# A two-layer hybrid decoder step on one core: small parameters as one row, the constant table in two parts, and the first weights of layer 0 by halves of their rows

## The chip, the core and the metric

The kernel runs on one core of a Trainium2 chip. The core has TensorE (PE, with its weight loads PEld), VectorE (DVE), ScalarE (ACT), GpSimd (POOL) and SyncE (SP), and 16 DMA engines that move data between device memory and the on-chip memories. SP and POOL also issue transfers: each has a queue of its own, and transfers of one queue are issued in the order of the program. The metric is the time of one execution on the device, in microseconds (us).

## The reference

Two decoder layers run over 256 prompt tokens and 8 sample tokens, model width 1024, all in float32. In each layer one wide projection `u = x @ w_in` feeds three token mixers (retention, state-space, sliding-window attention). Gates from the same `u` mix their results, an output projection, a layer norm and a gated feed-forward block follow. What the change touches is the start of the first layer: which columns of `w_in` are used there, and the small vectors of one number per head.

```python
(q_r, k_r, v_r, g_r, z, xbc, dt_raw, q_c, k_c, v_c, gates) = split(x @ w_in)
dt = softplus(dt_raw + dt_bias);  a = -exp(a_log)          # 16 heads
y  = ssd(...) + d_skip[:, None] * xs                       # 16 heads
# sliding-window attention: 8 query heads, 2 key heads of 64, window 128
bias   = rel_bias[t5_bucket(max(dist, 0))]                 # 32 buckets x 8 heads
logits = where(mask, q_c . k_c / 8 + bias, -1e30)
p = softmax(concat([logits, sinks], -1))[..., :-1];  o_c = p @ v_c
```

## The kernel before

The 264 token columns lie along the free dimension: `x` is kept transposed as eight blocks of 128 rows by 264 columns. Since products in full float32 are wanted, each float32 operand is split into a rounded part and a rest (`xh`, `xl` for the data, `wh`, `wl` for the weights), and each block product is three matmuls (`mm3`): wh by xh, wh by xl, wl by xh, each 128x128 weights by 264 columns. One output block of 128 columns of `w_in` (a unit, PSUM tile `ps_u`) is 8 blocks, so 24 matmuls.

Weights come in strips of 1 MB (256 columns of `w_in`, two units) on SP's queue (`strip`), into a pool of four buffers. For each unit `wsplit` makes `wh` on ACT (line 139, a rounded copy) and `wl` on DVE (line 144, a subtraction). Small loads go on POOL's queue (`ld`, line 167).

Layer 0 starts like this. `load_x` loads the first 128 columns of the constant table `cst` (an identity matrix) and x; PE transposes x by blocks (`ps_x`, line 127), ACT and DVE split each block (`xsplit`). Then come the units in this order: `w_kv` (2 units: keys and values of the attention), `w_qc` (4 units: its queries), `w_v` (4 units), `w_qk` (8 units). The strips of `w_qc` are gathered by two head groups each, so each strip is two transfers of 0.5 MB with runs of 128 numbers (512 bytes). The rest of `cst`, 1.1 MB, is loaded on SP's queue behind `w_qc` and ahead of `w_v` (`load_const`). `params` loads the vectors of a layer: 100 rows of 128 numbers (`par_rows`), which PE transposes at once (`ps_par`), and the vectors of one number per head (`dt_bias`, `a_log`, `d_skip`, `sinks`) by broadcasting loads into 128 partitions (`head`). `params` of layer 1 runs early in layer 0's mixers.

The attention needs a bias table. `bias_table` builds 8 rows of 383 numbers in `brow`, from the 32x8 bucket table (matmul `ps_rb`), writes them to device memory (`bias_row`), copies them there into 128 shifted places per head (`bias`, two copies of 766 KB), and loads the shifted table back as `bias_t` (two loads of 512 KB). The score tiles `ps_sc` on PE are read by DVE (`lg<-ps_sc,bias_t`, line 156), which adds the bias; the score tiles come from a pool of four PSUM buffers (`psm`), so later score matmuls wait until DVE has read earlier ones.

The order on each engine is fixed when the program is built: a list scheduler sorts the instructions by the program's order, by priorities (`high_priority`) and by explicit "not before" links (`issue_after`). Some generators (bias table, attention, layer 1's parameters) are put on a list and advanced in pieces by `pump` between units.

Of the kernel before, what the change touches and what calls it, by code (L numbers as in the profile page):

```python
# [10 lines left out]
F32 = mybir.dt.float32  # L11
# [8 lines left out]
DEPTH = 2  # L20
# [10 lines left out]
NEG = -1e30  # L31
RSCALE = 128**-0.5
CONV = 1536

# [70 lines left out]
class Kern:  # L105
# [87 lines left out]

    def wsplit(self, raw, shape):

        n = int(np.prod(shape))
        pool = self.hps[self.nsplit % len(self.hps)]
        self.nsplit += 1
        h, l = (pool.tile([128, 1024], F32R, tag=t, bufs=3 if pool is self.hp else 1, name=t) for t in ("wh", "wl"))
# [11 lines left out]
        return hv, lv  # L211

    def mm3(self, ps, wh, wl, xh, xl, first, last):
# [14 lines left out]

    def gemm_kouter(self, ws, x, pss):
        n = len(x)  # L230
        for k in range(n):
            for (wh, wl), ps in zip(ws, pss):
                self.mm3(ps, wh[:, k], wl[:, k], x[k][0], x[k][1], k == 0, k == n - 1)


    def load_x(self):
        nc, a, cp = self.nc, self.a, self.cp
        keep = _OFF["onehot"][0]
        self.cst = cp.tile([128, keep], F32, name="cst")
        nc.sync.dma_start(self.cst[:, 0:128], a["cst"][:, 0:128])  # L240

# [6 lines left out]
        nc.sync.dma_start(xt[1], a["x_prompt"][0, 128:256])  # L248
        nc.sync.dma_start(xs, a["x_sample"][:, 0])
        bias = self.bias_table()  # L250
# [11 lines left out]
        self.neg = cp.tile([128, 128], F32R, name="neg")  # L262
# [4 lines left out]
        nc.vector.memset(self.neg.bitcast(F32), -1.0 / 128)  # L267
        nc.vector.memset(self.eps[:, 0:1], EPS)
        nc.vector.memset(self.eps[:, 1:2], 4.0 * EPS)

    def load_const(self):
        nc, a = self.nc, self.a
        keep = _OFF["onehot"][0]
        nc.sync.dma_start(self.cst[:, 128:], a["cst"][:, 128:keep])
        self.par = [None] * DEPTH

    def params(self, l):

        nc, a, cp = self.nc, self.a, self.cp
        rows = self.T2("par_rows")[:100, :128]  # L280
        q = self.ld
# [12 lines left out]
        q(hd[:, 16:32], a["a_log"][l].partition_broadcast(128))  # L294
        for s in range(2):
            q(
                hd[s * 64 : s * 64 + 64, 32:40],
                a["d_skip"][l].rearrange("(h s) -> s h", s=2)[s].partition_broadcast(64),
            )
        q(hd[:, 40:48], a["sinks"][l].partition_broadcast(128))  # L300
        self.act(hd[:, 16:32], hd[:, 16:32], AF.Exp)
        self.par[l] = (t, hd)
# [242 lines left out]
    def mixers(self, l):  # L545
# [9 lines left out]

        def units(c0, n, name, done, kouter=False, unnormed=False):
            for i in range(0, n, 2):
                raw = self.strip([(0, 128, self.win(l, c0 + i * 128, 256))], (8, 256), name)
                if unnormed:
                    for u in range(2):  # L560
                        done(i + u, self.unnormed(self.wsplit(ucol(raw, u), (8, 128)), u > 0))
                    continue
                if kouter and i == 0:
                    ws = [self.wsplit(ucol(raw, u), (8, 128)) for u in range(2)]
                    pss = [self.pg("ps_u") for _ in range(2)]
                    self.gemm_kouter(ws, self.x, [p[:, :T] for p in pss])
                    for u in range(2):
                        done(u, pss[u])
                    continue
# [9 lines left out]

        kv = self.kv = self.E2("kv")  # L580
        units(KC, 2, "w_kv", lambda u, ps: self.act(kv[:, u * T : (u + 1) * T], ps[:, :T]), l == 0, l > 0)
        qc = self.qc = self.E4("qc")
        wq = a["w_in"][l][:, QC : QC + 512].rearrange("(k p) (g c) -> p k g c", p=128, g=2)
        for i in range(2):
# [5 lines left out]
            if l == 0 and i == 1:  # L590
                self.load_const()
                self.params(0)
            for u in range(2):
                t = 2 * i + u
                w = self.wsplit(raw[:, :, :, u * 64 : (u + 1) * 64], (8, 2, 64))
                if l > 0:
                    ps = self.unnormed(w)
                else:
                    ps = self.pg("ps_u")
                    self.gemm(w, self.x, ps[:, :T])  # L600
                self.act(qc[:, t * T : (t + 1) * T], ps[:, :T])
                self.pump(1)
# [3 lines left out]
        self.ld(rd, self.win(l, DT, 16))  # L606
        self.conv_prep(l)
        self.rate = 1.5
        vr = self.vr = self.E4("vr")
        put = lambda u, ps: self.act(vr[:, u * T : (u + 1) * T], ps[:, :T])  # L610
        units(VR, 2, "w_v", put, False, l > 0)
        if l > 0:
# [463 lines left out]
    def swa(self, l):  # L1076
# [97 lines left out]
        KT3 = KT[:, :1024].rearrange("p (b n) -> p b n", b=8)  # L1174
        self.ld(kc3, a["cache_swa_k"][l].rearrange("b w g d -> w b (g d)"))
        self.ld(vc3, a["cache_swa_v"][l].rearrange("b w g d -> w b (g d)"))
# [74 lines left out]
    def ret(self, l):  # L1251
# [37 lines left out]
        def load_state(h):  # L1289
            s0 = self.SI("rs0")[:, :1024]  # L1290
            self.ld(s0.rearrange("p (b v) -> p b v", b=8), a["state_ret"][l][:, h].rearrange("b k v -> k b v"))
            loaded.append(s0)
# [352 lines left out]
```

## Time and profile before

| | us |
|---|---|
| three timed runs | 1118.53, 1124.67, 1124.10 |
| their median | 1124.1 |
| the profiled execution | 1120.48 |
| its span, from the first to the last instruction | 1118.7 |
| around the span (1120.48 less 1118.7) | 1.8 |
| PE busy | 1085.1 (97%) |
| DVE, ACT, POOL busy | 838.8, 660.8, 165.6 |

The profile is of one execution. Busy times of the engines overlap. The granted clock of TensorE in the profiled execution is 0.988 of full speed as a mean. The chain of work that ended last is followed back from the last instruction; 89% of it are PE's instructions.

### The profile page before, as it was taken

The numbers are of one execution on the slowest core, as the hardware profiler recorded it, in microseconds if no ns is written. First come the engines' busy times: TensorE is split into PE (matmuls) and PEld (weight loads), VectorE is DVE, ScalarE is ACT, GpSimd is POOL, SyncE is SP. The second block draws the span as 40 slices with busy tenths as digits, with TensorE's granted clock in tenths as the row PEclk, the third lists the DMA queues.
The fourth block names the chain that finished last, engine by engine and source line by source line (L and its number), as shares of the span: only waits on it lengthen the run. The fifth ranks groups of instructions, "written<-read, shape, count | busy, mean of one in ns | idle before, by whom it ended". The sixth has DMA issues, their size and how long they took to land.

```text
span 1118.7 us, 22107 instructions
## 1 busy us (share of the span) xinstructions
PE 1085.1 (97%) x8583; PEld 1032.6 (92%) x8583; DVE 838.8 (75%) x1898; ACT 660.8 (59%) x1318; POOL 165.6 (15%) x250
## 2 busy tenths in 40 slices
PE   6799999999999999999999999999999999999998
PEld 5788899998899999999998899989899999999996
DVE  3178685688968998777699769668886799777654
ACT  3147553767664686664457855456666558766452
POOL 5010001242000101222011000133100000122300
PEclk9889999999999999999999999999999999999999
DMA  9874445588455668899775445659766536889941
GB/s 212 217 259 151 130 138 167 187 218 260 144 188 156 193 219 287 288 299 336 223 229 173 152 138 153 173 145 273 213 189 203 171 122 223 286 290 306 323 177 40
DMA packets 179977, 230.78 MB, mean 206 GB/s; under 512 B 8056, under 2 KB 156160, under 8 KB 179696
## 3 DMA queue, kind: packets, MB, share of 16 engines
q1 hardware_dynamic: 159472, 166.95, 47.2%
q0 software_dynamic: 20336, 62.39, 19.7%
q8 instruction: 67, 1.10, 0.4%
q14 instruction: 38, 0.31, 0.1%
q10 hardware_dynamic: 64, 0.03, 0.0%
HBM read 213.57 MB, written 19.61 MB: 208 GB/s over the span
## 4 chain that ended last, share of the span: by engine, by line
PE 89%; DVE 4%; DMA 4%; ACT 2%; issue 1%; SPq 0%; ACTq 0%
PE ps_u L123 18%; PE ps_gate L123 13%; PE ps_fd L123 11%; PE ps_fg L123 9%; PE ps_fu L123 9%; PE ps_br L123 8%; PE ps_z L123 5%; PE ps_o L123 4%; DMA w_v<-in_w_in_dram 3%; PE ps_y L123 2%; DVE wl L144 1%; PE ps_po L123 1%; ACT wh L139 1%; PE ps_var L123 1%; DVE xl L156 1%
## 5 line engine op out<-in xcount | busy, mean ns | idle before, releaser
L123 PE MATMUL ps_u<-xh,wh 128*128 128x264 f32 x608 | 179.0, 296 | 9.9 <-ACT wh L139 9.9
L123 PE MATMUL ps_u<-xl,wh 128*128 128x264 f32 x608 | 177.4, 292 | 0.0
L123 PE MATMUL ps_u<-xh,wl 128*128 128x264 f32 x608 | 176.6, 293 | 0.5 <-DVE wl L144 0.5
L123 PEld LDWEIGHTS ps_u<-xh,wh 128*128 128x128 f32 x608 | 117.6, 194 | 15.1 <-ACT wh L139 11.3
L123 PEld LDWEIGHTS ps_u<-xh,wl 128*128 128x128 f32 x608 | 117.7, 194 | 3.7 <-issue 1.8
L123 PEld LDWEIGHTS ps_u<-xl,wh 128*128 128x128 f32 x608 | 117.9, 194 | 2.6 <-issue 2.1
L123 PE MATMUL ps_gate<-xh,wh 128*128 128x264 f32 x384 | 111.2, 293 | 4.5 <-ACT th L139 3.2
L123 PE MATMUL ps_gate<-xh,wl 128*128 128x264 f32 x384 | 110.6, 291 | 0.0
L123 PE MATMUL ps_gate<-xl,wh 128*128 128x264 f32 x384 | 110.1, 290 | 0.0
L123 PE MATMUL ps_fd<-fh,wl 128*128 128x264 f32 x352 | 100.4, 285 | 0.0
L123 PE MATMUL ps_fd<-fh,wh 128*128 128x264 f32 x352 | 100.3, 285 | 0.0
L123 PE MATMUL ps_fd<-fl,wh 128*128 128x264 f32 x352 | 100.1, 284 | 0.0
L144 DVE TENSOR_TENSOR wl<-w_fd,wh 128x1024 fp32r<-128x1024 f32 (+1 forms) x48 | 54.2, 1135 | 38.6 <-ACT wh L139 38.3
L123 PE MATMUL ps_fg<-xh,wh 128*128 128x264 f32 x288 | 82.1, 285 | 0.6 <-DVE v L156 0.6
L123 PE MATMUL ps_fg<-xl,wh 128*128 128x264 f32 x288 | 82.5, 286 | 0.0
L123 PE MATMUL ps_fu<-xh,wh 128*128 128x264 f32 x288 | 82.5, 286 | 0.0
L167 POOL DMA_DIRECT2D s<-in_state_ssm_dram x32 | 28.7, 898 | 361.0 <-ACT sn L139 223.7
L123 PE MATMUL ps_fu<-xl,wh 128*128 128x264 f32 x288 | 82.1, 285 | 0.0
L123 PE MATMUL ps_fg<-xh,wl 128*128 128x264 f32 x288 | 81.8, 284 | 0.0
L123 PE MATMUL ps_fu<-xh,wl 128*128 128x264 f32 x288 | 81.8, 284 | 0.0
L139 ACT ACTIVATE wh<-w_gate 128x1024 fp32r<-128x1024 f32 x48 | 50.7, 1059 | 48.4 <-PE ps_br L123 17.8
L139 ACT ACTIVATE wh<-w_fd 128x1024 fp32r<-128x1024 f32 (+1 forms) x48 | 47.2, 986 | 53.7 <-PE ps_fd L123 44.6
(454 smaller groups left out, 3431.9 us busy)
## 6 DMA issues: line engine op xcount, KB each, us to landing
w_gate<-in_w_in_dram SPq DMA_DIRECT2D x24, 1024.0 KB, 5.5
w_fg<-in_w_ffn_gate_dram SPq DMA_DIRECT2D x22, 1024.0 KB, 5.3
w_fu<-in_w_ffn_up_dram SPq DMA_DIRECT2D x22, 1024.0 KB, 5.6
s<-in_state_ssm_dram POOLq DMA_DIRECT2D x32, 512.0 KB, 7.0
w_fd<-in_w_ffn_down_dram SPq DMA_DIRECT2D x16, 1024.0 KB, 9.4
out_dram<-sn POOLq DMA_DIRECT2D x24, 512.0 KB, 7.7
w_qk<-in_w_in_dram SPq DMA_DIRECT2D x8, 1024.0 KB, 5.2
w_xs<-in_w_in_dram SPq DMA_DIRECT2D x8, 1024.0 KB, 5.3
```

The costliest lines, as they stand in the source:

```text
L123: return self.nc.tensor.matmul(out, lhsT, rhs, start=start, stop=stop).ins
L139: i = self.nc.scalar.activation(out=out, in_=in_, func=func, scale=scale, **kw)
L144: return self.nc.vector.tensor_tensor(out=out, in0=a, in1=b, op=op).ins
L156: return self.nc.vector.scalar_tensor_tensor(out=out, in0=a, scalar=s, in1=b, op0=op0, op1=op1).ins
L167: return self.nc.gpsimd.dma_start(out, in_).ins
```

## The change

- **Vectors per head.** `params` no longer loads `dt_bias`, `a_log`, `d_skip` and `sinks` by broadcast. Four loads of 16, 16, 16 and 8 numbers put them into one row beside `par_rows`; one matmul of a row of ones with that row (`ps_head`) spreads them over 128 partitions, and ACT copies them out into `head`. Layer 1's `params` now runs near the end of layer 0.
- **Constant table.** The first load takes 256 columns (identity and ones) instead of 128; the rest is loaded later in the program's text, in SP's queue still behind `w_qc` and ahead of `w_v`.
- **First weights by halves of rows.** In layer 0, `w_kv` and `w_qc` are loaded as two strips each that hold rows 0 to 511 and 512 to 1023: two of 0.5 MB with 1 KB runs, two of 1 MB with 2 KB runs. `wsplits` splits 512 numbers a row at a time into halves of a `wh`/`wl` pair. All units of a strip's first half run before its second half.
- **Warm-up.** 32 matmuls of 128x128 on a constant tile (`neg`) are put on PE ahead of the transposes.
- **Splits of x.** They get a priority of 400. The bias row is pumped after all eight blocks of x, with `issue_after` links that put the loads of the retention state (`rs`) behind the load of the key cache.

```diff
+WARM = 32
@@ load_x
-        nc.sync.dma_start(self.cst[:, 0:128], a["cst"][:, 0:128])
+        nc.sync.dma_start(self.cst[:, 0:256], a["cst"][:, 0:256])
...
+        ps = self.pg("ps_warm")
+        for _ in range(WARM):
+            self.mm(ps[:, :128], self.neg, self.neg)
...
         for k in range(KB):
-            if k == KB - 1:
-                self.pump(1)
...
-            self.xsplit(*self.x[k], ps[:, :T])
+            with self.tc.high_priority(400):
+                self.xsplit(*self.x[k], ps[:, :T])
+        self.pump(1)
@@ params
-        q(hd[:, 0:16], a["dt_bias"][l].partition_broadcast(128))
...
+        row = slot[:1, 128:184]
+        for nm, o, n in (("dt_bias", 0, 16), ("a_log", 16, 16), ("d_skip", 32, 16), ("sinks", 48, 8)):
+            q(row[:, o : o + n], a[nm][l : l + 1])
+        ph = self.pm("ps_head")
+        self.mm(ph[:, 0:56], self.c("ones")[0:1], row)
@@ wsplits, new
+        t = [self.hp.tile([128, 1024], F32R, tag=t, bufs=3, name=t) for t in ("wh", "wl")]
+        return [self.wsplit(r, shape, tuple(x[:, i * n : (i + 1) * n] for x in t)) for i, r in enumerate(raws)]
@@ halves, new
+            pss = [self.pg("ps_u") for _ in range(n)]
+            for i in range(2):
+                raw = self.strip([(0, 128, self.win(l, c0, n * 128)[:, 4 * i : 4 * i + 4])], (4, n * 128), name)
+                for u in range(0, n, 2):
+                    ws = self.wsplits([pieces(raw, u + v) for v in range(2)], shape)
+                    if n == 2:
...
+                                self.mm3(pss[v][:, :T], *(w[:, k] for w in ws[v]), *x, i + k == 0, i == 1 and k == 3)
...
+                        self.gemm(ws[v], self.x[4 * i : 4 * i + 4], pss[u + v][:, :T], i == 0, i == 1)
@@ mixers, layer 0
+            for u, ps in enumerate(halves(KC, 2, "w_kv", ucol, (4, 128))):
+                put_kv(u, ps)
...
+            pss = halves(QC, 4, "w_qc", head, (4, 2, 64))
+            self.params(0)
@@ load_state
+            with self.tc.issue_after(self.kv_ld):
+                self.ld(s0.rearrange("p (b v) -> p b v", b=8), a["state_ret"][l][:, h].rearrange("b k v -> k b v"))
```

On ACT, at the very start of the program, before:

```order
L139 ACTIVATE xh<-ps_x 128x264 x5
L139 ACTIVATE wh<-w_kv 128x1024 x2
L139 ACTIVATE xh<-ps_x 128x264 x2
L139 ACTIVATE wh<-w_qc 128x1024
L139 ACTIVATE xh<-ps_x 128x264
```

and in the same place now:

```order
L141 ACTIVATE wh<-w_kv 128x512 x4
L141 ACTIVATE xh<-ps_x 128x264 x4
L141 ACTIVATE wh<-w_qc 128x512 x2
L141 ACTIVATE xh<-ps_x 128x264 x4
L141 ACTIVATE wh<-w_qc 128x512 x2
```

All four copies of `w_kv` stand ahead of the first `xh`, and two copies of `w_qc` ahead of the other four; before, five of the eight `xh` stood ahead of any weights. DVE has its subtractions in the same order.

On POOL's queue, behind the last row of `par_rows`, before (`head_313` is layer 0's, `head_4391` layer 1's):

```order
L167 DMA head_313<-in_d_skip_dram 64x8x1 x2
L167 DMA head_313<-in_sinks_dram 128x8
L167 DMA w_dt<-in_w_in_dram 128x8x16
L167 DMA cst_rows<-in_state_conv_dram 24x1536
...
L167 DMA rs_1629<-in_state_ret_dram 128x8x128
L167 DMA rs_1840<-in_state_ret_dram 128x8x128
L167 DMA head_4391<-in_dt_bias_dram 128x16
L167 DMA bias_row<-brow 8x383
L167 DMA head_4391<-in_a_log_dram 128x16
L167 DMA head_4391<-in_d_skip_dram 64x8x1 x2
L167 DMA head_4391<-in_sinks_dram 128x8
L167 DMA bias<-bias_row 512x1x383 x2
```

and in the same place now, up to the load of the key cache and the states:

```order
L169 DMA par_rows<-in_d_skip_dram 1x16x1
L169 DMA par_rows<-in_sinks_dram 1x8x1
L169 DMA w_dt<-in_w_in_dram 128x8x16
L169 DMA cst_rows<-in_state_conv_dram 24x1536
...
L169 DMA bias_row<-brow 8x383
L169 DMA bias<-bias_row 512x1x383 x2
L169 DMA bias_t<-bias 128x4x256 x2
L169 DMA kcache<-in_cache_swa_k_dram 128x8x128
L169 DMA rs_1679<-in_state_ret_dram 128x8x128
L169 DMA rs_1890<-in_state_ret_dram 128x8x128
```

Layer 1's broadcast loads and the loads of the states no longer stand ahead of the bias row and the bias copies.

On PE, around the score tiles of the third and fourth head, before (`ps_u_663` is the second unit of `w_qk`):

```order
L123 MATMUL ps_u_663<-xh_84,wl_660 128x264
L123 MATMUL ps_sc_547<-kv_169,qc_232 128x128
L123 MATMUL ps_sc_547<-kv_169,qc_232 128x256
L123 MATMUL ps_u_663<-xh_84,wh_659 128x264
L123 MATMUL ps_sc_548<-kv_169,qc_232 128x128
```

and now (`ps_u_571` and `ps_u_611` are the third and the fourth unit of `w_v`):

```order
L125 MATMUL ps_u_571<-xh_84,wl_568 128x264
L125 MATMUL ps_sc_597<-kv_202,qc_203 128x128
L125 MATMUL ps_sc_597<-kv_202,qc_203 128x256
L125 MATMUL ps_sc_598<-kv_202,qc_203 128x128
L125 MATMUL ps_sc_598<-kv_202,qc_203 128x256
L125 MATMUL ps_u_611<-xh_84,wh_607 128x264
```

The fifth and sixth score tile, which take buffers that DVE must first have read with the bias table, moved from 93 matmuls of `ps_u` behind the first eight score matmuls to 24 behind them.

## Rows read from the trace of the kernel before

**Rows 1.** The page, busy time, share of the span and instructions of each engine.

```profile
PE 1085.1 (97%) x8583; PEld 1032.6 (92%) x8583; DVE 838.8 (75%) x1898; ACT 660.8 (59%) x1318; POOL 165.6 (15%) x250
```

**Rows 2.** The chain that ended last, in order of time: start us, us, what.

```profile
20.50 34.49 DMA w_v<-in_w_in_dram
...
60.26 13.19 PE ps_u L123 x93
...
417.09 2.95 PE ps_fu L123 x24
```

**Rows 3.** PE's timeline: start us, us, instruction [idle before <-releaser].

```profile
12.03 0.59 PE L123 MATMUL ps_u<-xh,wh 128*128 128x264 f32 x1
...
28.37 0.39 PE L123 MATMUL ps_u<-xh,wh 128*128 128x264 f32 x1 [3.63 <-ACT wh L139]
...
45.35 0.59 PE L123 MATMUL ps_u<-xh,wh 128*128 128x264 f32 x1 [5.54 <-ACT wh L139]
...
56.78 1.43 PE L123 MATMUL ps_sc<-kv,qc 64*128 64x128 f32 x6 [1.70 <-ACT convbuf L139]
```

**Rows 4.** Stretches: PE, PEld, DVE, ACT, POOL busy (instructions), PEclk, DMA share, GB/s.

```profile
30.00:35.00 5.00, 5.00 (x31) 5.00 (x30) 1.06 (x3) 0.13 (x2) 1.05 (x1) 0.68 1.11 176
45.00:50.00 5.00, 4.20 (x17) 3.89 (x18) 2.45 (x2) 1.80 (x4) 0.00 (x0) 0.50 0.59 214
55.00:60.00 5.00, 3.12 (x15) 1.86 (x14) 3.66 (x13) 4.81 (x10) 1.38 (x3) 0.71 1.06 345
60.00:70.00 10.00, 10.00 (x68) 9.81 (x67) 4.06 (x4) 2.77 (x5) 3.25 (x5) 0.81 0.94 324
8.00:10.00 2.00, 1.37 (x8) 0.93 (x8) 1.45 (x4) 1.27 (x5) 1.16 (x3) 1.00 1.13 347
14.00:16.00 2.00, 2.00 (x11) 2.00 (x10) 1.50 (x4) 1.06 (x1) 2.00 (x3) 1.00 1.39 92
18.00:20.00 2.00, 2.00 (x18) 2.00 (x17) 0.31 (x1) 0.01 (x1) 0.54 (x1) 1.00 0.80 0
50.00:52.00 2.00, 2.00 (x18) 1.96 (x17) 0.00 (x0) 0.00 (x0) 0.00 (x0) 0.94 0.53 190
```

**Rows 5.** ACT's timeline, columns as in rows 3: splits of the weights.

```profile
10.74 2.00 ACT L139 ACTIVATE wh<-w_kv 128x1024 fp32r<-128x1024 f32 x2 [0.39 <-DMA w_kv<-in_w_in_dram]
...
27.26 1.06 ACT L139 ACTIVATE wh<-w_qc 128x1024 fp32r<-128x1024 f32 x1 [4.73 <-DMA w_qc<-in_w_in_dram]
...
44.24 1.06 ACT L139 ACTIVATE wh<-w_v 128x1024 fp32r<-128x1024 f32 x1 [14.12 <-DMA w_v<-in_w_in_dram]
...
55.09 1.06 ACT L139 ACTIVATE wh<-w_v 128x1024 fp32r<-128x1024 f32 x1 [8.29 <-DMA w_v<-in_w_in_dram]
```

**Rows 6.** SP's timeline, the time its queue took to issue (SPq).

```profile
2.98 9.15 SPq L191 DMA_DIRECT2D w_qc<-in_w_in_dram  x4
12.17 5.32 SPq L274 DMA_DIRECT2D cst<-in_cst_dram  x1
17.53 9.83 SPq L188 DMA_DIRECT2D w_v<-in_w_in_dram  x2
```

**Rows 7.** Transfers issued by POOL: count, KB each, median us from issue to landing.

```profile
head<-in_d_skip_dram POOLq DMA_DIRECT2D x1, 2.0 KB, 15.8
...
bias_row<-brow POOLq DMA_DIRECT2D x1, 12.0 KB, 14.5
...
bias<-bias_row POOLq DMA_DIRECT2D x1, 766.0 KB, 20.9
...
bias_t<-bias POOLq DMA_DIRECT2D x2, 512.0 KB, 6.8
```

**Rows 8.** POOL's timeline, columns as in rows 3: the steps of the bias table.

```profile
18.80 0.54 POOL L167 DMA_DIRECT2D bias_row<-brow  x1 [2.65 <-DVE xl L144]
...
33.95 2.26 POOL L167 DMA_DIRECT2D bias<-bias_row  x2 [5.54 <-DMA bias_row<-brow]
...
60.81 1.56 POOL L167 DMA_DIRECT2D bias_t<-bias  x2
```

More of the change, by code (lines that the diff above doesn't have):

```diff
@@ L192, in strip, with wsplit @@
         return v
-    def wsplit(self, raw, shape):
+    def wsplit(self, raw, shape, into=None):
         n = int(np.prod(shape))
-        pool = self.hps[self.nsplit % len(self.hps)]
-        self.nsplit += 1
-        h, l = (pool.tile([128, 1024], F32R, tag=t, bufs=3 if pool is self.hp else 1, name=t) for t in ("wh", "wl"))
+        if into is None:
+            pool = self.hps[self.nsplit % len(self.hps)]
+            self.nsplit += 1
+            into = tuple(pool.tile([128, 1024], F32R, tag=t, bufs=3 if pool is self.hp else 1, name=t) for t in ("wh", "wl"))
+        h, l = into
         spec = {2: "p (a b) -> p a b", 3: "p (a b c) -> p a b c"}[len(shape)]
@@ L249, in load_x @@
         nc.sync.dma_start(xs, a["x_sample"][:, 0])
+        self.neg = cp.tile([128, 128], F32R, name="neg")
+        nc.vector.memset(self.neg.bitcast(F32), -1.0 / 128)
+        self.par = [None] * DEPTH
+        ps = self.pg("ps_warm")
+        for _ in range(WARM):
+            self.mm(ps[:, :128], self.neg, self.neg)
         bias = self.bias_table()
@@ L554, in unit, with halves, units @@
             return ps
-        def units(c0, n, name, done, kouter=False, unnormed=False):
+        def halves(c0, n, name, pieces, shape):
+            pss = [self.pg("ps_u") for _ in range(n)]
[4 more added lines that the diff above has]
+                    if n == 2:
+                        for k in range(4):
+                            for v in range(2):
+                                x = self.x[4 * i + k]
+                                self.mm3(pss[v][:, :T], *(w[:, k] for w in ws[v]), *x, i + k == 0, i == 1 and k == 3)
+                        continue
+                    for v in range(2):
+                        self.gemm(ws[v], self.x[4 * i : 4 * i + 4], pss[u + v][:, :T], i == 0, i == 1)
+            return pss
+        def units(c0, n, name, done, unnormed=False):
             for i in range(0, n, 2):
@@ L561, in units @@
                         done(i + u, self.unnormed(self.wsplit(ucol(raw, u), (8, 128)), u > 0))
[L562 to L568, printed above, removed]
                     continue
@@ L580, in mixers @@
         kv = self.kv = self.E2("kv")
-        units(KC, 2, "w_kv", lambda u, ps: self.act(kv[:, u * T : (u + 1) * T], ps[:, :T]), l == 0, l > 0)
+        put_kv = lambda u, ps: self.act(kv[:, u * T : (u + 1) * T], ps[:, :T])
         qc = self.qc = self.E4("qc")
+        put_qc = lambda t, ps: self.act(qc[:, t * T : (t + 1) * T], ps[:, :T])
         wq = a["w_in"][l][:, QC : QC + 512].rearrange("(k p) (g c) -> p k g c", p=128, g=2)
-        for i in range(2):
+        if l == 0:
+            for u, ps in enumerate(halves(KC, 2, "w_kv", ucol, (4, 128))):
+                put_kv(u, ps)
+            head = lambda raw, t: raw.rearrange("p k (g t d) -> p k g t d", g=2, t=4)[:, :, :, t]
+            pss = halves(QC, 4, "w_qc", head, (4, 2, 64))
+            self.params(0)
+            for t, ps in enumerate(pss):
+                put_qc(t, ps)
+                self.pump(1)
+        else:
+            units(KC, 2, "w_kv", put_kv, True)
+        for i in range(2 if l else 0):
             raw = self.strip(
@@ L589, in mixers @@
             )
-            if l == 0 and i == 1:
-                self.load_const()
-                self.params(0)
             for u in range(2):
[L594 to L601, printed above, removed]
+                put_qc(2 * i + u, self.unnormed(self.wsplit(raw[:, :, :, u * 64 : (u + 1) * 64], (8, 2, 64))))
                 self.pump(1)
@@ L607, in mixers @@
         self.conv_prep(l)
+        if l == 0:
+            self.load_const()
         self.rate = 1.5
@@ L610, in mixers @@
         put = lambda u, ps: self.act(vr[:, u * T : (u + 1) * T], ps[:, :T])
-        units(VR, 2, "w_v", put, False, l > 0)
+        units(VR, 2, "w_v", put, l > 0)
         if l > 0:
```

30 lines of the change are left out of this document (11 added, 19 removed).

## The prediction

> **What bounds the kernel now.** I read the page first: PE is busy 97% of the span [rows 1], so only PE's gaps and its slow stretches are to be had. The chain in order of time says where they lie [rows 2]: one wait for `w_v` fills it from 20.50 to 54.99, and from about 60 us on PE runs almost without a break. So the change, which rewrites the first 60 us and a few instructions of layer 1, is worth what PE loses before that.
>
> PE's timeline gives the idle part [rows 3]: 3.63 us before 28.37 (second strip of `w_qc`, whose split starts at 27.26), 5.54 before 45.35 (first strip of `w_v`, split from 44.24 [rows 5]) and 1.70 before 56.78, where the score matmul waits for a buffer that ACT empties late, behind a split that waits for the second `w_v` strip (55.09 [rows 5]). Together 10.9 us.
>
> The clock gives the other part. At the full level 24 matmuls of a unit take 2.95 us [rows 2], 0.123 each. After each of the gaps the granted clock fell, to 0.50 of 2.4 GHz, that is 1.2 GHz, in parts of the stretches shown [rows 4]: 31 matmuls in 30 to 35 where 41 would fit (1.2 us lost); 17 in 4.20 busy us in 45 to 50 (2.1 lost); 3.12 busy us at a mean of 0.71 in 55 to 60 (0.9); 68 in 60 to 70 where 81 would fit (1.7). Sum 5.9 us. What is recoverable behind the start is thus 10.9 + 5.9 = **16.8 us**.
>
> Why do the strips come late? Not by their size. The transfers run at 347 GB/s in 8 to 10, then at 92 in 14 to 16 and at 0 in 18 to 20 with the engines still 80% busy [rows 4]. In that time the broadcast loads were in flight: 2 KB of `d_skip`, 512 elements of 4 bytes each with a stride of two, take up to 15.8 us to land [rows 7]. SP itself needed 9.15 us to issue the four transfers of `w_qc`, 5.32 for the table, 9.83 for two `w_v` strips [rows 6]. So I take the small-element loads to be what held the strips; the trace doesn't separate them from the 512-byte runs of `w_qc`, and the change removes both.
>
> **The change part by part.**
>
> *Vectors as a row, and `w_qc` by halves.* Four broadcast loads go, and the four of layer 1 leave this stretch. Bytes ahead of and with the first `w_v` strip on SP's queue: x 1.1 MB, table 0.13 and 1.1, `w_kv` 1.05, `w_qc` 2.1, strip 1.05: 6.5 MB. At 324 GB/s (60 to 70 [rows 4]) that is 20 us, at 285 it would be 23, and 2 us pass before the first transfers: with both: the first `w_v` strip is there at 22 to 25 instead of 44.24. The second half of `w_qc` comes at about 18. PE reaches `w_v` at about 35 (below), so 10 us of cover stand over the first wait: 3.63 and 5.54 go in full. If the flow stayed as bad as 92 GB/s for another 6 us, the cover would still hold. New on PE: one `ps_head` matmul, on ACT four more evacuations of 8 to 16 columns; ACT is idle 14.12 us before 44.24 [rows 5], so nothing for these.
>
> *`w_kv` by halves, splits behind weights.* The code puts the splits of x first by priority, but the order now has ACT do all four `w_kv` copies first, and they need the second half of `w_kv`. A copy of a whole unit takes about 1.0 us (2.00 for two [rows 5]), half a unit about 0.5. The same 1 MB lands as before, about 10.7 [rows 5]; two half copies more, one `xh`: first `ps_u` at about 12.3 against 12.03 [rows 3]. Bounds: 11.5, if the halves land earlier, to 14; I take **0.3 us lost**. Four blocks of x stay behind the first `w_qc` half (about 14.6, copies until 15.7): PE has 24 matmuls at the slow spacing to run by then (5 us, until 17.5), so no wait.
>
> *Warm-up.* 32 matmuls of 128 columns at no more than 0.22 us each (the spacing of a 264-column matmul there) are 7.2 us from about 1, done by 8.2; the transposes begin then, but ACT takes the first `xh` now only at about 12, and the last transpose needed for it is done by 11.5. Cost 0 for that, up to 0.5 if the memset is late. Gain: in 14 to 16 PE did 11 matmuls in 2 us and in 18 to 20 it did 18 [rows 4], so the start runs at the lower level, 18 matmuls from 12.03, 1.8 us lost. After the gap of 3.63 us the clock fell again [rows 3, 4]; between the end of the warm-up and 12.3 PE has only transposes with gaps. By the row nothing is left of the warmth: I take 0, range 0 to 1.8. The Trainium skill ("TensorE: Matmul & The Clock Gate", "What's actually happening") says that the slow state is the default and that activity lifts it, by which the warm-up would be worth the 1.8 us; no run here shows that yet.
>
> *Second `w_v` strip and the emptying of buffers.* In the new order PE's transposes of k and v for the sample rows (`ps_cts`), between the first and second unit of `w_v`, wait for a buffer that ACT empties behind its third `w_v` copy, so behind the second `w_v` strip. That strip landed 10.85 us after the first (55.09 less 44.24 [rows 5]), while the bias copies ran; by the same distance it is there at 33 to 36, at a stretch with worse flow (190 GB/s at a share of 0.53 in 50 to 52 [rows 4]) at 38. PE is through the first unit at 38.2. A copy of 1.06 and one small evacuation follow: **1.0 us lost**, bounds 0 and 4. The wait of 1.70 before 56.78 goes in exchange.
>
> *Bias row early, states late.* This edit pays nothing by itself and creates a new wait. The row is written at about 18.8 as before [rows 8], behind all splits of x; it took 14.5 us to land [rows 7] with the broadcast and state loads ahead, now perhaps 5.5: about 24.4. The copies then took 20.9 [rows 7]. They move 3.1 MB both ways, 14.5 us at the 214 GB/s of 45 to 50 [rows 4]. So `bias` lands at 39 to 45 and `bias_t` 6.8 us later [rows 7] plus issue, at 46.5 to 54. But the third and fourth heads' score tiles now stand on PE between the third and the fourth unit of `w_v` and need buffers that DVE frees with `bias_t`. PE gets there at about 46. Queued behind that wait on PE: the fourth `w_v` unit and all of `w_qk`; on DVE, behind the same bias table, the second `w_qk` subtraction. I take `bias_t` at 47.5: **1.5 us lost**, bounds 0 and 8, with the clock's fall afterwards 0 to 2.
>
> *Rest.* Layer 1's parameters at the end of layer 0, and states after the key cache: small orders in stretches where PE runs on other work; 0, bounds -0.5 and +2.
>
> **The sum.** PE: first unit 12.3, `w_kv` done 21.8 (with the four transposes and the bias-row matmuls inside), `w_qc` 96 x 0.123 later, 34, transposes 35.3, first `w_v` unit 38.2, wait 1.0, second 42, eight score matmuls, third 46, wait 1.5, fourth, scores, first `w_qk` unit about 55; 21 matmuls of the next, 57.8. Before, that point was 73.45 (60.26 + 13.19, 93 matmuls after the scores [rows 2]), with 0.9 us of score matmuls not yet done: this way 16 us. By losses: 16.8 removed, less 0.3, 1.0 and 1.5: 14.0. I go by the second, which is the surer, with half a microsecond of the first: 14.5. The profiled execution of 1120.48 less 14.5 is **1106**. Against the median of the runs, 1124.1, which lies 3.6 above it, the same gain would give 1109.6; the profile's own execution is between the three, so I stay with 1106 and let the range hold the other.
>
> **The rivals.**
>
> 1. *The bias table is late.* The copies take 20.9 us again or more, since the weight strips now flow beside them: `bias_t` at 53 to 55, PE waits 7 to 9 us at the fifth score tile and runs slowly for some us after it. Gain 14.5 - 7 = 7: **1113 to 1115**. For it: a share of 0.53 at 190 GB/s, far from full flow [rows 4]; against it: the state loads are behind. The Trainium skill ("DMA: Bandwidth & Descriptors", "Rules for kernel authors") says that a transfer whose outermost dimension is smaller than 16, as a broadcast's, is confined to that many engines. By that the copies with an outermost 4 would use 4 of 16 engines and their time would not shorten with a free queue: it would be the 20.9 and this rival. The share of 0.53 agrees without proving it.
>
> 2. *Slower, not faster.* The bias table comes no earlier than before, and PE now stands before the fifth score tile until it does. Break-even is a landing at 47.5 + 14.5 = 62; before, `bias_t` landed at about 60.81 + 6.8 = 67.6 [rows 7, 8], when the score tiles that need it stood later on PE. At 67.6 the loss is 5.6 us, and a fall of the clock behind so long a gap adds 1 to 3 (2.1 in 45 to 50): **1126 to 1129**. It needs `bias` 36 us after its copies are issued at 24.4, against 20.9: strips and copies would have to hold each other up on the same engines.
>
> 3. *Clock up early and no new waits.* The warm-up lifts the first stretch (1.8), the `ps_cts` and `bias_t` waits are 0 (2.5), the first unit starts with the half strip (0.8): 14.5 + 5 = 19.5, **1099 to 1101**.
>
> 4. *It doesn't do what it says.* The weights' strips stay late, since not the small elements but the rest held them: SP's table load still stands ahead of `w_v` with 5.32 us of issue. `w_v` at 38, say, leaves a wait of 3 us and a slow stretch of 2: **1111**.
>
> **How the numbers follow.** Forecast 1102 to 1110: 0.52. Rival 1 0.18, rival 2 0.06, rival 3 0.14, rival 4 0.10. The range leaves out rival 2 and the outermost of 1 and 3: 1098 to 1117. Within 0.5% (5.6 us, about what a measurement of this kernel can tell from no change) means 1118.5 to 1129.7 of the median: rival 2 in part and a tail of 1, 0.07; slower by more, rival 2's upper end on a run that lies at the median, 0.03; faster 0.90.
>
> **What would show it.** Right: first `w_v` split at 22 to 26 on ACT's timeline, no PE gap over 1 us from 13 to 38, `d_skip` landing in the row within 6 us, the only gaps at `ps_cts` and at the fifth score tile, under 3 us each. Wrong: a gap of over 4 us before that tile with `bias_t` as what DVE waits for (rival 1), `w_v` later than 33 (rival 4), the first stretch at 0.12 per matmul (rival 3), or new gaps in layer 1, which I have put at nothing.

## The result and the profile after

The changed kernel took 1106.1 us (median of four runs, 1103.6 to 1113.0) beside 1121.4 us for the kernel before (four runs, 1118.5 to 1124.7): a ratio of 0.987 with a 95% interval of 0.983 to 0.992. The profiled execution took 1103.6 us with a span of 1101.8, which is 16.9 us less than the span before.

The page's first part reads now (beside [rows 1]; busy time, share of the span, instructions):

```profile
PE 1085.3 (99%) x8619; PEld 1034.5 (94%) x8619; DVE 841.1 (76%) x1904; ACT 663.8 (60%) x1332; POOL 163.5 (15%) x248
```

PE's work is the same to 0.2 us, although 7.1 us of it is now the warm-up; the span is shorter because PE stands still less and runs more of it at the full clock. PE's waits from 12 to 345 us, longest first (what waits, for whom: us in total, times, longest), before:

```profile
PE ps_u L123 <- ACT wh L139: 9.2, 2, 5.5
PE ps_br L123 <- DVE zt L156: 2.7, 1, 2.7
PE ps_gate L123 <- ACT th L139: 1.8, 1, 1.8
PE ps_sc L123 <- ACT convbuf L139: 1.7, 1, 1.7
PE ps_gate L123 <- DVE dte L144: 1.4, 1, 1.4
```

and after:

```profile
PE ps_sc L125 <- DVE lg L158: 1.7, 1, 1.7
PE ps_u L125 <- ACT xh L141: 1.3, 1, 1.3
PE ps_gate L125 <- ACT th L141: 1.1, 1, 1.1
PE ps_rso L125 <- DMA rs<-in_state_ret_dram: 0.8, 1, 0.8
```

The two waits for the weight strips, 9.2 us, are gone, as is the one for `convbuf`. In their place stands one of the two new waits that the prediction named, the score matmul behind `lg`, which adds the bias table: 1.7 us. The other, at `ps_cts`, isn't there. The 1.3 us for `xh` end at 11.98, at the first unit, which began at 12.03 before [rows 3]. And something changed that the prediction didn't speak of: of the waits for `zt`, `th` and `dte`, which lie at 157 to 288 us, two are gone and the one for `th` went from 1.8 to 1.1 us.

Three timelines of the changed kernel show the start of the chain (start us, us, instruction [idle before <-releaser]): PE's first unit and its wait at the fifth score tile, ACT's first and third split of `w_v`, DVE's first use of the bias table.

```profile
11.98 0.59 PE L125 MATMUL ps_u<-xh,wh 128*128 128x264 f32 x1 [1.29 <-ACT xh L141]
...
50.29 1.45 PE L125 MATMUL ps_sc<-kv,qc 64*128 64x128 f32 x8 [1.73 <-DVE lg L158]
```

```profile
30.19 1.06 ACT L141 ACTIVATE wh<-w_v 128x1024 fp32r<-128x1024 f32 x1 [1.79 <-PE ps_u L125]
...
36.08 1.06 ACT L141 ACTIVATE wh<-w_v 128x1024 fp32r<-128x1024 f32 x1 [0.95 <-PE ps_u L125]
```

```profile
49.36 0.29 DVE L158 SCALAR_TENSOR_TENSOR lg<-ps_sc,bias_t 128x128 f32<-128x128 f32 x1 [3.20 <-DMA bias_t<-bias]
```

ACT's splits of `w_v` wait for PE now (for a free buffer), no longer for the strips as in [rows 5]: the strips are there first. What DVE waits for at 49.36 is the landing of `bias_t`.

Stretches of the changed kernel (columns as in [rows 4]) show the flow of the transfers at the start, the wait with the slow clock behind it, and the rest of layer 0:

```profile
12.00:20.00 8.00, 7.93 (x35) 6.12 (x35) 4.75 (x11) 3.37 (x9) 0.88 (x4) 1.00 1.04 326
...
45.00:50.00 5.00, 3.56 (x29) 3.01 (x26) 1.64 (x3) 1.51 (x3) 4.91 (x7) 1.00 1.07 390
50.00:55.00 5.00, 4.71 (x25) 4.37 (x26) 4.11 (x12) 0.00 (x0) 0.63 (x2) 0.73 1.03 324
75.00:345.00 270.00, 267.42 (x2147) 250.04 (x2147) 210.09 (x534) 163.69 (x337) 36.77 (x61) 1.00 0.58 176
```

and the first and the last of these stretches in the kernel before, with the one in which its clock fell:

```profile
12.00:20.00 8.00, 8.00 (x45) 7.26 (x45) 4.72 (x7) 2.92 (x6) 4.69 (x9) 1.00 1.12 95
...
275.00:300.00 25.00, 22.25 (x157) 19.67 (x156) 23.41 (x60) 14.60 (x30) 3.54 (x7) 0.93 0.42 136
75.00:345.00 270.00, 264.05 (x2113) 246.77 (x2110) 207.87 (x539) 166.38 (x351) 35.71 (x58) 0.99 0.58 174
```

Between 12 and 20 us the transfers move 326 GB/s instead of 95, at about the same busy share of the DMA engines (1.04 and 1.12). Between 75 and 345 us PE is idle 2.6 us instead of 6.0, and a fall of the clock (0.93 over 25 us, 1.7 us of time) is gone. The first matmul of the output projection, a point at which both orders agree, stands at 343.00 before and at 324.58 after:

```profile
343.00 0.28 PE L123 MATMUL ps_o<-mh,wh 128*128 128x264 f32 x1
```

```profile
324.58 0.28 PE L125 MATMUL ps_o<-mh,wh 128*128 128x264 f32 x1
```

So 18.4 us had been won by then. Of these, 3.4 + 1.7 = 5.1 were won behind 75 us, and 13.3 in the start. Some 1.5 us were lost again later, which leaves the 16.9. Of these, 1.1 lie in the program's last 21 us, the same work in both kernels but for two records, at a lower granted clock after the change (0.81 beside 0.92). Before and after:

```profile
1098.00:1118.70 20.70, 15.96 (x117) 11.20 (x115) 8.68 (x20) 5.35 (x12) 1.26 (x1) 0.92 0.14 53
```

```profile
1080.00:1101.80 21.80, 17.62 (x119) 12.17 (x117) 8.99 (x20) 5.34 (x12) 1.26 (x1) 0.81 0.14 51
```

### The profile page after: what moved, and what is told of

Its sections match the earlier page's. It is cut to its first block, busy times and chain, and to the rows that moved or that the text cites. A ratio compares the mean times of both kernels' runs of the same rounds, so it can differ in the third digit from the quotient of the medians.

```text
span 1101.8 us, 22210 instructions
## 1 busy us (share of the span) xinstructions
PE 1085.3 (99%) x8619; PEld 1034.5 (94%) x8619; DVE 841.1 (76%) x1904; ACT 663.8 (60%) x1332; POOL 163.5 (15%) x248
## 3 DMA queue, kind: packets, MB, share of 16 engines
q1 hardware_dynamic: 156384, 166.95, 47.5%
## 4 chain that ended last, share of the span: by engine, by line
PE 78%; issue 11%; DVE 4%; DMA 4%; ACT 1%; POOL 1%; POOLq 0%; ACTq 0%
PE ps_gate L125 13%; PE ps_fd L125 11%; PE ps_u L125 10%; PE ps_fg L125 9%; PE ps_fu L125 9%; PE ps_br L125 8%; PE ps_z L125 5%; PE ps_o L125 4%; PE ps_y L125 2%; DMA bias<-bias_row 2%; DVE wl L146 1%; PE ps_var L125 1%; PE ps_st L125 1%; DMA rs<-in_state_ret_dram 1%; ACT wh L141 1%
## 5 line engine op out<-in xcount | busy, mean ns | idle before, releaser
L125 PE MATMUL ps_u<-xh,wh 128*128 128x264 f32 x608 | 176.7, 293 | 2.5 <-ACT xh L141 1.3
L125 PEld LDWEIGHTS ps_gate<-xh,wh 128*128 128x128 f32 x384 | 72.9, 191 | 5.6 <-ACT th L141 2.8
```

The costliest lines, as they stand in the source:

```text
L125: return self.nc.tensor.matmul(out, lhsT, rhs, start=start, stop=stop).ins
```

## The experiments

Each edit is against the changed kernel, where nothing else is said. Ratios are to the kernel before, on the same chip as the run, so rows are compared by their ratios and not by their medians; the last three columns are of the profiled execution: GB/s from 12 to 20 us, start of the first `w_v` split, and the idle time before the fifth score tile.

| | median us | ratio (95% interval) | GB/s | `w_v` split | idle |
|---|---|---|---|---|---|
| before | 1121.4 | 1 | 95 | 44.2 | none |
| changed | 1106.1 | 0.987 (0.983 to 0.992) | 326 | 30.2 | 1.7 |
| e3 head vectors by broadcast | 1117.8 | 0.998 (0.996 to 1.000) | 146 | 40.0 | 6.7 |
| e4 `w_qc` strips as before | 1104.2 | 0.986 (0.983 to 0.989) | 291 | 33.4 | none |
| e6 before + row of vectors | 1101.5 | 0.984 (0.980 to 0.988) | 257 | 30.3 | none |
| e10 before + `d_skip` alone as a row | 1105.5 | 0.987 (0.984 to 0.991) | 243 | 30.1 | none |
| e11 before + the other three as a row | 1122.6 | 1.002 (0.999 to 1.004) | 103 | 45.2 | none |
| e1 wide bias copies | 1101.8 | 0.983 (0.980 to 0.987) | 330 | 30.1 | none |
| e2 no warm-up | 1103.3 | 0.984 (0.981 to 0.986) | 337 | 28.4 | 1.8 |
| e5 wide copies, no warm-up | 1100.4 | 0.983 (0.979 to 0.986) | 333 | 27.3 | none |
| e7 states ahead of the bias row | 1107.8 | 0.989 (0.985 to 0.993) | 340 | 32.9 | none |
| e8 the changed kernel again (one execution) | 1102.8 | | 333 | 33.7 | none |
| e9 before + row + wide copies | 1099.9 | 0.984 (0.980 to 0.987) | 264 | 29.1 | none |

**Which part brings the strips early?** The prediction had taken the loads of small elements for it and said that the trace couldn't tell them from the 512-byte runs of `w_qc`. First the two parts were undone one at a time. e3:

```diff
-        row = slot[:1, 128:184]
-        ... four loads into the row, ps_head, five copies by ACT
+        q(hd[:, 0:16], a["dt_bias"][l].partition_broadcast(128))
+        ... a_log, d_skip (twice, "(h s) -> s h"), sinks, as in the kernel before
```

> The changed kernel with the vectors per head loaded by the broadcast loads of before, for both layers; all else as changed (halves, warm-up, table parts). Layer 1's loads stand again ahead of the bias row on POOL's queue. Theory A (the loads of 4-byte elements held the strips): DMA runs under 150 GB/s somewhere between 12 and 22 us, the first w_v split comes after 33 instead of 30.2 or later, d_skip takes over 8 us to land, the bias table comes 5 to 10 us later than in the changed kernel; time 1110 to 1116. Rival B (the 512-byte runs of w_qc held them): rates stay above 250 GB/s to 22 us, first w_v strip landed by 26, time within 3 us of the changed kernel.

Nearly all of the gain went, with the halves and all else in place. The flow fell to 146 GB/s and the first `w_v` split waited for its strip:

```profile
40.03 1.06 ACT L141 ACTIVATE wh<-w_v 128x1024 fp32r<-128x1024 f32 x1 [8.55 <-DMA w_v<-in_w_in_dram]
```

The bias table was late too: PE's waits from 12 to 75 us begin with 6.7 us at the fifth tile.

```profile
PE ps_sc L125 <- DVE lg L158: 6.7, 1, 6.7
PE ps_u L125 <- ACT qc L141: 1.3, 1, 1.3
```

This is the prediction's first rival, in the kernel in which broadcast loads stand ahead of the bias row. e3's time lies above the 1110 to 1116 that were expected. e4:

```diff
-            pss = halves(QC, 4, "w_qc", head, (4, 2, 64))
+            for i in range(2):
+                raw = self.strip([(0, 128, wq[:, :, :, i * 128 : (i + 1) * 128])], (8, 2, 128), "w_qc")
+                ... two units of each, by whole rows
+                if i == 0: self.params(0); self.pump(2)
```

> The changed kernel with w_qc loaded and split as before (two strips of 256 columns, each as two transfers of 0.5 MB with 512-byte runs); w_kv by halves, the row of vectors and the rest as changed. Theory A (the loads of 4-byte elements held the strips): rates over 200 GB/s all through 8 to 24 us, the first w_v strip is there before PE wants it at 37, no wait of PE on a wh split above 1 us, time within 3 us of the changed kernel. Rival B (the 512-byte runs held them): a wait of PE for the second w_qc or the first w_v strip of 3 us or more with a slow stretch behind it, time 1109 to 1115.

Theory A held: 291 GB/s, and the first `w_v` split waits for PE, not for its strip. (In its one profile the clock rose late, see e8; the 3.5 us so lost came back at the score tile, where it had no wait.) Then each part alone, on the kernel before. e6 takes only the row and the first 256 columns of the table:

```diff
-        nc.sync.dma_start(self.cst[:, 0:128], a["cst"][:, 0:128])
+        nc.sync.dma_start(self.cst[:, 0:256], a["cst"][:, 0:256])
...
+        row, ps_head and five copies by ACT in params, as in the change
```

> The kernel before with only the vectors per head as one row for both layers (and 256 columns in the first part of the table, which the row of ones needs). No halves, no warm-up, bias row and states in the order of before. Theory A (the row is what brings the strips early): first w_v strip there by 30 instead of 44.24, no wait of PE for w_qc or w_v above 1 us, time 1103 to 1109. Rival B (the halves and the order of the queues carry half of it): a wait for w_qc's second strip of 2 us or more stays, time 1110 to 1115. For the later stretch: if the two waits of PE at 157 (1.5 us) and at 289 (2.7 us and a slow stretch) are still there, they belong to the order that the rest of the change makes; if they are gone, to the row.

The row alone brings as much as the whole change (0.984 beside 0.987, with intervals that overlap), and 1.5 us more than was expected of it. Neither wait for strips is left in the start; from 12 to 345 us PE's longest are these:

```profile
PE ps_u L123 <- DVE wl L144: 1.2, 1, 1.2
PE ps_u L123 <- ACT wh L139: 1.2, 2, 0.8
PE ps_gate L123 <- ACT th L139: 1.2, 1, 1.2
```

The waits of before for `dte` and `zt`, at 157 and 288 us, are gone here as well, and in e3 too, where the row is undone and the rest is there. But the stretch as a whole isn't mended by the row: from 75 to 345 us PE is idle 5.3 us in e6, against 6.0 before, 2.6 in the changed kernel and 3.5 in e3, since the waits above, all behind 80 us, stand in the place of the old ones. e6 and then e3:

```profile
75.00:345.00 270.00, 264.74 (x2109) 246.76 (x2108) 205.16 (x526) 162.66 (x342) 36.89 (x61) 0.99 0.59 174
```

```profile
75.00:345.00 270.00, 266.47 (x2148) 249.22 (x2146) 209.84 (x539) 165.17 (x353) 35.20 (x58) 1.00 0.60 178
```

Last, which of the four vectors. `d_skip` is taken apart by even and odd heads, so its loads have a stride of two and runs of 4 bytes, 512 to a load and 1024 to a layer; the others have runs of 32 or 64 bytes, one for each of 128 partitions. e10 makes a row of `d_skip` alone, e11 of the other three:

```diff
 e10
-        for s in range(2): q(hd[s * 64 : s * 64 + 64, 32:40], a["d_skip"][l]...[s].partition_broadcast(64))
+        q(row, a["d_skip"][l : l + 1]); self.mm(ph[:, 0:16], self.c("ones")[0:1], row)
+        for s in range(2): self.act(hd[s * 64 : s * 64 + 64, 32:40], ph[s * 64 : s * 64 + 64, s:16:2])
 e11
-        q(hd[:, 0:16], ...dt_bias); q(hd[:, 16:32], ...a_log); q(hd[:, 40:48], ...sinks)
+        three loads into row, ones x row, three copies by ACT; d_skip as before
```

> The kernel before with d_skip alone as a row of 16 numbers, for both layers; dt_bias, a_log and sinks by broadcast as before. Theory A (it is the 1024 elements of 4 bytes of the four d_skip loads, not the 128 short rows of the others, that held the strips): rates over 150 GB/s all through 12 to 24 us, w_v's first split not waited for longer than 2 us, time 1100 to 1107, as e6. Rival B (all broadcast loads of short rows together): w_v's first strip at 33 or later, time 1109 to 1116.

> The counterpart of e10: the kernel before with dt_bias, a_log and sinks as a row, d_skip by its four broadcast loads as before. Theory A: rates under 100 GB/s in most of 14 to 20 us as before, w_v's first split awaited until 36 to 44, time 1111 to 1119. Rival B: half of e6's gain, w_v at 30 to 35, time 1107 to 1111.

The stretch from 12 to 20 us of both, e10 and then e11, settles it:

```profile
12.00:20.00 8.00, 8.00 (x46) 7.09 (x47) 4.75 (x7) 2.95 (x6) 4.64 (x10) 1.00 1.12 243
```

```profile
12.00:20.00 8.00, 8.00 (x32) 6.41 (x33) 4.89 (x7) 3.71 (x7) 5.73 (x11) 1.00 1.18 103
```

With `d_skip`'s loads of 2 KB the flow is 103 GB/s, and e11 is no faster than before (3.6 us above the range that was expected). How so few bytes hold so many shows in what each queue took of the 16 engines' time in these 8 us (packets, MB, share). For POOL's queue, in the kernel before, in e11 and in e10:

```profile
q0 software_dynamic: 112, 0.02, 73.1%
```

```profile
q0 software_dynamic: 143, 0.00, 75.9%
```

```profile
q0 software_dynamic: 381, 0.79, 47.8%
```

With `d_skip` by broadcast, 0.02 MB or less fill three quarters of the engines' time. Whether the other three vectors bring a little on top of `d_skip` can't be told (0.984 for e6 beside 0.987 for e10). In e11 `d_skip`'s loads took 18.0 us from issue to landing (median of four); as a row in the changed kernel the same numbers took 4.8:

```profile
head<-in_d_skip_dram POOLq DMA_DIRECT2D x4, 2.0 KB, 18.0
```

```profile
par_rows<-in_d_skip_dram POOLq DMA_DIRECT2D x1, 0.1 KB, 4.8
```

The Trainium skill ("DMA: Bandwidth & Descriptors", "Rules for kernel authors") says that a strided last dimension becomes one descriptor per element and should be made contiguous. These runs agree with the advice (the count of descriptors isn't shown here), and add what such loads cost the other transfers: e10 and e11 lie 17 us apart.

**The wait for the bias table.** e1 writes the copies with another dimension outermost:

```diff
-            self.ld(self.bias[h : h + 4], once[h : h + 4].unsqueeze(1).to_broadcast([4, 128, 383]))
+            self.ld(self.bias[h : h + 4].rearrange("h p c -> p h c"), once[h : h + 4].unsqueeze(0).to_broadcast([128, 4, 383]))
```

> The changed kernel, with the two bias copies in device memory written with the 128 shifted places outermost instead of the four heads; bytes, run length (1532 bytes) and all orders stay. Theory A (the copies are confined to few engines by their outermost dimension of four, and PE's gap of 1.73 us at the fifth score tile is the late bias table): the copies land 7 to 9 us after their issue at 26.7 instead of 15.5 to 16.7, bias_t is there by 42, the gap before 50.3 is gone and with it the slow stretch behind it (15 matmuls at 0.22 instead of 0.123 us, 1.5 us): about 3.2 us less, some 1100 beside a profiled 1103.6. Rival B (the copies are bound by their packets, or by the strips beside them): they still take 14 to 17 us, the gap stays at 1.5 to 2 us, no difference. Rival C: the faster copies hold the w_v and w_qk strips, a new wait of PE on a wh split of 1 us or more between 35 and 60, no gain.

The copies (median of the two, issue to landing) in the changed kernel and in e1:

```profile
bias<-bias_row POOLq DMA_DIRECT2D x2, 766.0 KB, 16.1
```

```profile
bias<-bias_row POOLq DMA_DIRECT2D x2, 766.0 KB, 10.6
```

They take 5.5 us less, though not the 7 to 9 us that were expected, and the wait and the slow stretch behind it are gone; the output projection starts 4.0 us earlier (320.6 beside 324.6). The median is 1101.8, with an interval that still overlaps the changed kernel's. That so many bytes moved faster by their order alone is what the rule on 16 engines in the Trainium skill ("DMA: Bandwidth & Descriptors", "Rules for kernel authors"), which the prediction cited for its first rival, would give; the engines of the copies were not counted apart here, so the cause stays open.

**The warm-up.** e2 drops it:

```diff
-        ps = self.pg("ps_warm")
-        for _ in range(WARM):
-            self.mm(ps[:, :128], self.neg, self.neg)
```

> The changed kernel without the 32 warm-up matmuls. The order now has four splits of x ahead of the first split of w_kv on ACT and DVE, since the transposes are no longer behind the warm-up. Theory A (the warm-up leaves nothing of the clock, and it was what put the splits of x behind the weights): first ps_u at 9.8 to 10.6 us instead of 11.98, its first matmuls at 0.22 us as with the warm-up, end of the w_kv and w_qc units 1 to 2 us earlier, and the time 0 to 2 us less, since the bias table doesn't come earlier by as much. Rival B (the warm-up is what lets the clock up in the first stretch): full spacing of 0.123 comes 2 us or more later than the 18.2 of the changed kernel, time 1 to 2 us more.

The first unit starts no earlier, at 12.05, since the transposes of three more blocks of x now stand ahead of it on PE; so that number of the expectation failed. But they are then done, and the point after the `w_qc` units is reached at 34.2 instead of 36.0. The full spacing (0.123 us from one matmul of a unit to the next, the higher level of the clock) comes at the same time, 18.3 beside 18.2: the warm-up does nothing for the clock that this pair shows. One pair is little, since the same kernel can rise 8 us later (e8 below). But over all profiled executions the rise came at 17.4 to 26.1 us in the six with the warm-up and at 15.6 to 22.7 in the seven without, so nothing speaks for a gain. What it does is to delay the transposes, and with them to put the splits of x behind the weights. Of the 1.8 us, 1.4 are left at the feed-forward block; the wait at the fifth tile is still there, 1.8 us. The median, 1103.3, is lower than the changed kernel's, with intervals that overlap. Both edits together, e5:

> The changed kernel with both edits: bias copies with the 128 places outermost, and no warm-up. Theory A (the two gains are of different kinds and add): transposes of the parameters (ps_par) at about 34.3 as without the warm-up, against 36.0; no gap before the fifth score tile; layer 0's ps_o at about 319, that is 1.6 us ahead of e1 and 5.5 ahead of the changed kernel; time 0.1 to 0.2% below e1's median. Rival B (what the earlier start saves is given back at the bias table): a gap of 1 us or more before the fifth score tile, time as e1. Rival C (in a run where the clock rises only at about 25.5, as in e3 and e4, 3.4 us are lost again): first ps_u at full spacing after 25, ps_par at 37 to 38.

No gap at the tile, the point after `w_qc` at 33.1, and 1100.4 us: below e1, but not by more than the runs scatter. It and e9, the kernel before with the row and the wide copies alone, have the lowest medians here; by their ratios (0.983 and 0.984) they can't be told from e1, e2 and e6.

> The kernel before with the vectors as one row (as e6) and the bias copies with the 128 places outermost (as e1), nothing else. Theory A (with the fifth score tile 79 matmuls of ps_u behind the first eight, as in e6, PE has no gap there that a faster copy could take): time within 2 us of e6; the copies land in 8 to 10 us instead of 17 to 19. Rival B (the late table crowds DVE: the two waits of e6 for w_bc's splits at 82 and 84, 2.4 us, go when DVE adds the bias earlier): 2 to 3 us under e6, some 1098 to 1099, beside e5 the fastest.

e9's copies landed in 12.4 us instead of e6's 18.0, and e6's two waits at the `w_bc` splits are unchanged (1.2 and 1.2 us): theory A.

**The states behind the key cache.** e7 drops that link:

```diff
-            with self.tc.issue_after(self.kv_ld):
-                self.ld(s0.rearrange("p (b v) -> p b v", b=8), a["state_ret"]...)
+            self.ld(s0.rearrange("p (b v) -> p b v", b=8), a["state_ret"]...)
```

> The changed kernel without the link that holds the two loads of the retention state behind the key cache: they stand ahead of the bias row again, and the order puts the fifth score tile 72 matmuls behind the first eight instead of 24. Theory A (the link pays nothing by itself, it makes the tile early and the table early together): the table lands 4 to 10 us later, PE reaches the tile 9 us later, wait 0 to 3 us, time within 3 us of the changed kernel. Rival B (an early table is worth it): a wait of 4 us or more at the fifth tile, time 1108 or more.

The loads of `bias_t` were issued at 48 and 51 instead of 43 and 45, the fifth tile was computed at 56.7, with no wait. 1107.8 us, the same as the changed kernel within the intervals: the edit makes table and tile early together.

The link does something else that the expectation didn't ask for. Without it the stretch behind 75 us is much as it was before the change: PE is idle 3.7 us there instead of 2.6, its clock falls once more, to a mean of 0.77 from 185 to 200 us (3.4 us of time), and the output projection starts at 331.1 instead of 324.6, of which 2.7 us had been lost by the end of `w_qc` (38.7 beside 36.0). (This is its one profile, of the slowest of its four executions.)

```profile
75.00:345.00 270.00, 266.27 (x2109) 247.35 (x2108) 205.16 (x526) 163.56 (x347) 36.93 (x61) 0.99 0.58 174
185.00:200.00 15.00, 13.14 (x76) 11.49 (x77) 8.86 (x15) 9.32 (x18) 7.29 (x14) 0.77 0.34 91
```

All profiled executions divide in this way: the seven with the link (the changed kernel, e1 to e5, e8) have PE idle 2.3 to 3.5 us from 75 to 345 us and no fall of the clock there; the six without it (before, e6, e7, e9 to e11) have 3.7 to 6.0 us, and a fall in all but e11. The medians, over which other things vary, don't show it: e6 and e9 are without the link and among the fastest.

**When the clock rises.** e8 is the changed kernel once more.

> The changed kernel once more, unchanged. e4's PE ran the same instructions at the same times as the changed kernel's up to 18.2 us, and yet its matmuls went to the full spacing at 25.7, not at 18.2. Theory A (when the clock rises is not set by the kernel; one execution gets it some 7 us later than another): this run may show either 18 or 25 us; at 25 the start loses 3.4 us and the gap at the fifth score tile is gone, as in e4. Rival B (it is the halves of w_qc that bring the clock up): 18.2 again, gap of 1.7 again.

Theory A: its full spacing came at 26.1 us, not at 18.2. From 18 to 25 us, first the changed kernel, then the same kernel in e8:

```profile
18.00:20.00 2.00, 2.00 (x14) 1.53 (x13) 0.87 (x2) 0.78 (x2) 0.00 (x0) 1.00 0.95 267
20.00:25.00 5.00, 5.00 (x40) 4.74 (x39) 1.57 (x3) 2.36 (x6) 0.51 (x1) 1.00 1.10 351
```

```profile
18.00:20.00 2.00, 2.00 (x8) 1.51 (x8) 0.43 (x1) 0.61 (x2) 0.00 (x0) 1.00 0.94 281
20.00:25.00 5.00, 5.00 (x22) 4.33 (x22) 2.00 (x4) 1.32 (x3) 0.51 (x1) 1.00 1.07 343
```

The second column is the number of matmuls: 54 and 30. (No event of the clock is recorded before it first rises; a mean of 1.00 in such a stretch is no reading of it, and the spacing of 0.22 us is that of 1.2 GHz.) PE reached the point after `w_qc` at 39.5 instead of 36.0, and then had no wait at the score tile, since the table was there; its output projection started at 324.5 beside 324.6, and its time was 1102.8 beside 1103.6. In the changed kernel the table's wait and the clock at the start are thus one loss, not two: the one that comes last counts. Another chip isn't what it takes: e1 and e3 ran on the same chip, with the same order on PE up to there, and rose at 17.4 and 25.5.

## Why the prediction was right, and where it was not

**The term that carried it.** 16.8 us were to be had and 14.0 to be won in the start; 13.3 were. The waits for strips went in full. The first `w_v` strip took 12.8 us from an issue at 10.8 and was there at 23.6, in the 22 to 25 that were worked out from bytes. The sign named for it, a first split at 22 to 26 on ACT, was not met: the split came at 30.19, behind a buffer that PE freed, and cost PE nothing. Of the two causes that were left open, the small elements were right, and of them `d_skip` is enough by itself; `w_qc`'s runs were not (e4, e10, e11). One reading was off: the 15.8 us to land is that of a load for layer 1, issued at 26.4. The two in flight from 12 to 20 us took 10.3 (median):

```profile
head<-in_d_skip_dram POOLq DMA_DIRECT2D x2, 2.0 KB, 10.3
```

**The new waits.** At the fifth score tile 1.5 us were forecast at 46 to 47.5, and 1.73 were measured, ended at 50.29. The slow stretch behind it, which had only stood in the bounds (0 to 2), cost another 1.5: 15 matmuls at 0.22 us. At `ps_cts` 1.0 us was forecast and there was none: the second `w_v` strip was split at 36.08, after a wait for PE's buffer and not for the strip, before PE had done the first unit at 40.3. The first unit started 0.05 us earlier, not 0.3 later.

**Where the arrival times were off.** PE was through `w_qc` at 36.0, not 34. The slow spacing held to 18.2 and not to 16.4, and the transposes in between took that spacing too. e8 shows that this point moves between 18 and 26 from one execution to the next, with nothing in the kernel to set it.

**The warm-up.** Taking 0 for its gain, by the row and against the rule of the Trainium skill ("TensorE: Matmul & The Clock Gate", "What's actually happening"), was right: 7.1 us of matmuls without a gap, and the first units ran at the lower of the two levels all the same. Taking 0 for its cost was wrong, though the order printed ahead of the prediction shows the reason. I read there that the weights stand ahead of x, charged 0.3 us to the first unit, and didn't ask what had put them there. It cost 1.8 us at the end of `w_qc` in the one pair that shows it (e2).

**The step that failed.** "Rest", put at 0 with bounds of -0.5 and +2, brought 5.1 us between 75 and 345 us, outside its bounds. It was three waits of PE for ACT and DVE that the kernel before had, 5.9 us in all, of which 2.3 for similar ones remained, and a fall of the clock behind one of them. The part of "Rest" that this goes with is the states behind the key cache: with that link alone dropped, e7 lost 3.7 us to waits and 3.4 to the clock in this stretch, nearly as much as the kernel before (6.0 and 1.7). How the link does it is open, since any new order of the start took away the waits for `zt` and `dte` (e3, e6, e11), and without the link others came in their place.

**What was luck.** The 5.1 us made up for what the start fell short of and for the late 1.5 us. And the profiled execution won 16.9 us where 14.5 were forecast; that the median is 1106.1 and the forecast 1106 owes as much to four executions that lie between 1103.6 and 1113.0.

**The rivals.** The late table (rival 1) came true in e3 alone, with 6.7 us. Slower (rival 2) was never near; nor were late strips (rival 4). Rival 3's half, no wait at `ps_cts`, happened.

## What to carry to other kernels

A load with a strided last dimension of a few hundred 4-byte elements is not free because it is small: look at the GB/s of the stretch in which it is in flight, beside its DMA share, and load it as one contiguous row instead, to be spread by a matmul. When a change has many parts, run each alone: here one of them brought as much as all of them, and one, the warm-up, cost a little in the start. What speeds up the work ahead of a late transfer can be given back at the wait for it: a clock that rose 8 us sooner won 3.5 us up to the score tiles and nothing at the output projection (the changed kernel beside e8). So look after that transfer too.

## What was new about the hardware

The same program gets its full clock at 18.2 us in one execution and at 26.1 in another, with PE's instructions at the same times to 0.2 us up to there; over the runs of this case the rise lay between 15.6 (e9) and 26.1 (e8), and no run shows what sets it. A copy within device memory of 2 times 766 KB went from 16.1 to 10.6 us when its dimension of 128 stood outermost instead of that of 4. Two loads of 2 KB for each layer, with runs of 4 bytes, were worth 15.5 us of the whole kernel (e10 beside the kernel before on its chip, 1105.5 and 1121.0).
